# Start bytes of SBUF tiles within a 256-byte line, shifted for the inputs that TensorE streams through a four-layer fp32 network

## Chip, cores, metric

One core of one Trainium2 chip. The metric is device time in microseconds (us) of one execution, the median of several runs; lower is better.

## What is computed

Two layers of one kind and then two of another work on one sequence of 256 tokens with 1024 features. All tensors are float32. The matrix products are what costs time; cut to them, the reference is:

```python
# first kind of layer, DEPTH = 2
u = rms_norm(h, g_mix_pre)
(gq, gk, gv, gg, ra_f, ra_b, aq, ak, av, gate_a, gate_b) = jnp.split(u @ w_in, offsets, axis=-1)
branch_a = (o_gla * jax.nn.silu(gg)) @ w_o_gla
branch_b = gqa_attention(q, k, v) @ w_o_attn
mixed = jax.nn.sigmoid(gate_a) * branch_a + jax.nn.sigmoid(gate_b) * branch_b
h = h + rms_norm(mixed @ w_out, g_mix_post)
gate, up = jnp.split(rms_norm(h, g_ffn_pre) @ w_ffn_in, 2, axis=-1)      # 1024 -> 2 x 2816
h = h + rms_norm((jax.nn.silu(gate) * up) @ w_ffn_out, g_ffn_post)       # 2816 -> 1024
e = p_i @ w_ple_proj
h = h + rms_norm(jax.nn.sigmoid(h @ w_ple_gate) * e, g_ple_post)

# second kind of layer, DEPTH = 2
x = x + 0.5 * swiglu_ffn(rms_norm_2(x, ffn1_norm[i]), ffn1_w_in[i], ffn1_w_out[i])
proj = rms_norm_2(x, mix_norm[i]) @ w_in[i]
ya = (rg_lru(causal_dwconv(rx)) * jax.nn.gelu(rgate)) @ w_rnn_out[i]
yb = forgetting_attention(q, k, v, f_logit, ...) @ w_attn_out[i]
x = x + (jax.nn.sigmoid(ga + mb_a) * ya + jax.nn.sigmoid(gb + mb_b) * yb) @ w_o[i]
x = x + 0.5 * swiglu_ffn(rms_norm_2(x, ffn2_norm[i]), ffn2_w_in[i], ffn2_w_out[i])
x = x + jax.nn.sigmoid(rms_norm_2(x, ple_norm[i]) @ ple_w_gate[i] + ple_b_gate[i]) * (p[i] @ ple_w_proj[i])
```

## The kernel before

**Split products.** Every large product is computed in three matmuls of type float32r. Each operand is split into a rounded high part and a low remainder, and the kernel adds high x high, high x low and low x high. `weight` (L231) fetches 512 KB of weights into a tile `raw` and splits it into `hi` (ScalarE, L250) and `lo` (VectorE, L251), each 128 partitions x 1024 columns. Activations are split into pairs whose names end in h and l: `xTh`/`xTl` for a normalised input, `hh`/`hl` for the hidden units of an FFN, `oh`/`ol`, `yh`/`yl` and `mh`/`ml` in the mixers, `xrh`/`xrl` for the raw input of the last gate, `px` for the extra embedding.

**Two forms of product.** A matmul streams one operand (the moving one) past another that has been loaded into the array (the stationary one, 128 columns). In `gemm_fm` (L273, matmuls at L288 to L290) the weights are stationary and the activations move, 256 columns (1024 bytes of each partition) at a time. In `gemm_tm` (L297, matmuls at L315 to L317) the activations are stationary and the weights move, 512 columns at a time. Each matmul has a weight load of its own, and TensorE loads the stationary tile of the next matmul while the current one streams.

**Which layer uses which.** In the first two layers the FFN's first product is `gemm_fm` on `xT`, and the second is `gemm_tm` with `hh`/`hl` stationary. In the last two layers there are two FFNs each, both with `gemm_fm` in both products, so `hh`/`hl` move there. `layer_b` (L903) holds these four FFNs, `mixer_b` (L942) the mixer between them, `layer_a` (L518) the FFN of the first kind.

**Order.** Tiles are declared in pools, and a scheduling layer orders the instructions of each engine from dependencies and priorities. Nothing in this order is touched here.

**Where tiles start.** Pools are stacked in SBUF, and within a pool tiles follow each other. A tile's start byte in each partition is thus fixed when the program is built. `phase` (L212) puts a small unused tile at the head of a pool and pushes what follows by `n` bytes. Before the change, `act` (which holds `xT`) and `small` get 64 bytes each, and the pools of `layer_a`'s FFN and of `mixer_b` 32 bytes. With that, every moving or stationary activation pair starts at byte 0 of a 256-byte line (`px` at 224 in three places), while `raw`, `hi` and `lo` start at byte 192, all buffers of them. All these tiles are multiples of 256 bytes long, so each later block of them starts at the same byte of its line.

Of the kernel before, what the change touches and what calls it, by code (L numbers as in the profile page):

```python
# [11 lines left out]
F32 = mybir.dt.float32  # L12
# [6 lines left out]
P = 128  # L19
# [20 lines left out]
HOLD_B = 4  # L40
LAG = 3

X_PHASE = 64
POOL_PHASE = 32


class Norm:
# [3 lines left out]
    def __init__(self, net, g, tag="xT"):  # L51
        self.net, self.g = net, g
        self.xs = net.pair(net.act, tag)
        self.r = [None, None]
        self.R = net.act.tile([P, S], F32, tag="R", name=net.name("R"), bufs=2)
        self.ssq = [net.small.tile([P, 2], F32, tag="nssq", name=net.name("nssq")) for _ in range(2)]
# [124 lines left out]
class Net:  # L181
    def __init__(self, ctx, tc, a, raw_bufs=4, w_bufs=5, acc_bufs=3):
        self.tc = tc
        self.nc = tc.nc
        self.a = a
        pool = lambda name, bufs, **kw: ctx.enter_context(tc.tile_pool(name=name, bufs=bufs, **kw))
        psum = bass.MemoryType.PSUM
        self.const = pool("const", 1)
        self.wraw = pool("wraw", raw_bufs)
        self.whl = pool("whl", w_bufs)  # L190
        self.act = pool("act", 1)
        self.small = pool("small", 4)
        self.ps = pool("ps", acc_bufs, space=psum)
        self.pt = pool("pt", 2, space=psum)
        self.pm = pool("pm", 2, space=psum)
        self.pg = pool("pg", 1, space=psum)
        self.n = 0
        self.phase(self.act, X_PHASE)
        self.phase(self.small, X_PHASE)


        self.hold = self.held = None
        self.fetched = []
        nc = self.nc
        self.ident = self.const.tile([P, P], F32, name="ident")
        self.h = self.const.tile([P, 2, D], F32, name="h")
        self.expo = self.const.tile([P, 16], F32, name="expo")
        nc.vector.memset(self.expo, -0.5)
        self.ones = self.const.tile([P, P], F32, name="ones")
        nc.vector.memset(self.ones, 1.0)  # L210

    def phase(self, pool, n):  # L212

        pool.tile([P, n // 4], F32, tag="phase", name=self.name("phase"), bufs=1)

    def temporaries(self, ctx, bufs):
        self.tmp = ctx.enter_context(self.tc.tile_pool(name=self.name("tmp"), bufs=1))
# [300 lines left out]
def layer_a(net, i, nrm, following):  # L518
    nc, a, tc = net.nc, net.a, net.tc
    with ExitStack() as mx:  # L520
        nrm, px = mixer_a(net, i, mx, nrm)
    with tc.tile_pool(name=net.name("ffn"), bufs=1) as fp:
        net.phase(fp, POOL_PHASE)
        g_post = net.gain(a["g_ffn_post"][i])
        e = ple_proj(net, px, a["w_ple_proj"][i])
        raw = Raw(net, fp)
        net.ffn(nrm, a["w_ffn_in"][i], a["w_ffn_out"][i], net.post_norm(g_post, raw, fp, HOLD_FFN), fp)
        g_post = net.gain(a["g_ple_post"][i])
        nrm = following()
        px = ple_input(net, a["pT_2"][0]) if i + 1 == DEPTH else None  # L530

        def gated(tt, hf, acc):
            cs = slice(hf * 512, (hf + 1) * 512)
            t = net.t()
            nc.scalar.activation(t, acc, AF.Sigmoid)
            nc.vector.tensor_tensor(t, t, e[:, tt, cs], ALU.mult)
            return t

        net.gemm_tm(raw.xs, a["w_ple_gate"][i], net.post_norm(g_post, nrm, fp, HOLD_PLE if i + 1 < DEPTH else HOLD_LAST, gated), lag=LAG)
    return nrm, px  # L540


def ple_input(net, pT):
    with net.urgent(SPLIT_PRIO, 200):
        raw = net.t()
        net.nc.sync.dma_start(out=raw, in_=pT)
        px = (net.t((P, 2, S), F32R, "px"), net.t((P, 2, S), F32R, "px"))
        net.split_fm(raw, *px, 0)
    return px


def ple_proj(net, px, w):
    nc = net.nc
    e = net.t((P, 2, D), tag="e")
    net.gemm_tm(px, w, lambda tt, hf, acc: nc.scalar.copy(e[:, tt, hf * 512:(hf + 1) * 512], acc))
    return e
# [73 lines left out]
def flat(t):  # L630
    return t.rearrange("p a b -> p (a b)")


def blk(t, j):
    return t[:, 2 * j:2 * j + 2].rearrange("p a b -> p (a b)")
# [268 lines left out]
def layer_b(net, i, nrm, px, hT, following):  # L904
    nc, a, tc = net.nc, net.a, net.tc
    gains = a["gains"][i]
    gc = net.hp.tile([P, 48], F32, tag="gcols", name=net.name("gcols"), bufs=2)
    nc.sync.dma_start(out=gc, in_=gains)
    col = lambda k: gc[:, 8 * k:8 * k + 8]
    e = net.hp.tile([P, KB, S], F32, tag="e", name=net.name("e"))  # L910

    e_half = lambda px, q: net.gemm_fm(px, a["ple_w_proj_2"][i][q:q + 1], lambda j, acc: nc.scalar.copy(blk(e, 2 * q + j), acc), nkb=2)
    e_half(px, 0)
    with tc.tile_pool(name=net.name("ffn"), bufs=1) as fp:
        after = NormT(net, hT, col(1))
        net.ffn(nrm, a["ffn1_w_in_2"][i], a["ffn1_w_out_2"][i], net.add_scaled(hT, 0.5, after.blocks), fp, fm=True)
    with ExitStack() as cx:
        ms = mixer_b(net, i, cx, after)
        px = ple_input(net, a["pT_2"][i])
        nrm = NormT(net, hT, col(2))  # L920
        net.gemm_fm(ms, a["w_o"][i], net.add_scaled(hT, 1.0, nrm.blocks), tail=True)
    with tc.tile_pool(name=net.name("ffn"), bufs=1) as fp:
        e_half(px, 1)
        after = NormT(net, hT, col(3))
        net.ffn(nrm, a["ffn2_w_in_2"][i], a["ffn2_w_out_2"][i], net.add_scaled(hT, 0.5, after.blocks), fp, fm=True)
        nrm = following()
        px = ple_input(net, a["pT_2"][i + 1]) if i + 1 < DEPTH else None

        def epi(f, n, acc):
            t = net.t()[:, :n * S]  # L930
            net.times_r(t, acc, after)
            for c in range(n):
                nc.scalar.activation(t[:, c * S:(c + 1) * S], t[:, c * S:(c + 1) * S], AF.Sigmoid, bias=col(4)[:, f + c:f + c + 1])
            nc.vector.tensor_tensor(t, t, flat(e[:, f:f + n]), ALU.mult)
            nc.vector.tensor_tensor(flat(hT[:, f:f + n]), flat(hT[:, f:f + n]), t, ALU.add)
            nrm.blocks(f, n)

        net.gemm_fm(after.xs, a["ple_w_gate_2"][i], epi, tail=True)
    return nrm, px


def mixer_b(net, i, cx, nrm):  # L942
    nc, a, tc = net.nc, net.a, net.tc
    p1 = cx.enter_context(tc.tile_pool(name=net.name("mx"), bufs=1))
    net.phase(p1, POOL_PHASE)
    big = lambda tag, dt=F32: p1.tile([P, KB, S], dt, tag=tag, name=net.name(tag))
    fl = lambda t: t.rearrange("p a b -> p (a b)")
    xs, rs = nrm.xs, nrm.r
# [143 lines left out]
def _build(tc, a, out):  # L1092
    with ExitStack() as ctx:
        net = Net(ctx, tc, a)
        nc = tc.nc
        with ExitStack() as part:
            net.temporaries(part, T_BUFS_A)
            net.split = SPLIT_A
            nrm = lambda pool: first_norm(net, pool)
            nxt = [lambda: Norm(net, net.gain(a["g_mix_pre"][1])), lambda: Norm(net, net.gain(a["ffn1_norm_2"][0]))]  # L1100
            for i in range(DEPTH):
                nrm, px = layer_a(net, i, nrm, nxt[i])

        hp = ctx.enter_context(tc.tile_pool(name="hT", bufs=1))
        net.hp = hp
        net.temporaries(ctx, T_BUFS_B)
        net.split = SPLIT_B
        hT = hp.tile([P, KB, S], F32, name="hT")
        for tt in range(2):
            for hf in range(2):  # L1110
                ps = net.pt.tile([P, 4, P], F32, tag="pt", name=net.name("pt"))
                for j in range(4):
                    kb = hf * 4 + j
                    nc.tensor.transpose(ps[:, j], net.h[:, tt, kb * P:(kb + 1) * P], net.ident)
                nc.scalar.copy(hT[:, hf * 4:hf * 4 + 4, tt * P:(tt + 1) * P], ps)
        gc = hp.tile([P, 16], F32, name="gc")
        nc.sync.dma_start(out=gc, in_=a["gains_last"])
        nxt = [lambda: NormT(net, hT, gc[:, 0:8]), lambda: NormT(net, hT, gc[:, 8:16], out)]
        for i in range(DEPTH):
            nrm, px = layer_b(net, i, nrm, px, hT, nxt[i])  # L1120
# [140 lines left out]
```

## Time and profile before

| | us |
|---|---|
| median of 3 runs | 2344.41 |
| the 3 runs | 2346.03, 2344.41, 2343.48 |
| the profiled execution's own time | 2343.55 |
| its span, first to last instruction | 2341.8 |
| TensorE matmuls busy (16892) | 2291.4 |
| weight loads busy (16892) | 2168.4 |
| VectorE busy | 1600.6 |
| ScalarE busy | 1335.3 |
| GpSimd busy | 440.3 |

The span is 1.75 us shorter than the profiled execution's own time. A matmul's busy time of some 280 ns contains the pipeline behind the array and overlaps its successor, so the rate at which TensorE works is read from the distance between the starts of successive matmuls.

### The profile page before, as it was taken

The numbers are of one execution on the slowest core, as the hardware profiler recorded it, in microseconds if no ns is written. First come the engines' busy times: TensorE is split into PE (matmuls) and PEld (weight loads), VectorE is DVE, ScalarE is ACT, GpSimd is POOL, SyncE is SP. The second block draws the span as 40 slices with busy tenths as digits, with TensorE's granted clock in tenths as the row PEclk, the third lists the DMA queues.
The fourth block names the chain that finished last, engine by engine and source line by source line (L and its number), as shares of the span: only waits on it lengthen the run. The fifth ranks groups of instructions, "written<-read, shape, count | busy, mean of one in ns | idle before, by whom it ended". The sixth has DMA issues, their size and how long they took to land.

```text
span 2341.8 us, 42188 instructions
## 1 busy us (share of the span) xinstructions
PE 2291.4 (98%) x16892; PEld 2168.4 (93%) x16892; DVE 1600.6 (68%) x2133; ACT 1335.3 (57%) x2105; POOL 440.3 (19%) x443
## 2 busy tenths in 40 slices
PE   7999999998999999999999999999999999999997
PEld 6899899777899998799999899999999998999997
DVE  7876766477867765766586867665765677766655
ACT  6875554467764644554457765444644457755444
POOL 5222211064302110211001302110111103112101
PEclk9999999999999999999999999999999999999999
DMA  7445566554455666555665545666566655556662
GB/s 250 147 153 160 179 203 186 178 164 148 145 162 173 204 189 185 171 168 187 187 183 184 158 150 185 185 193 187 174 188 184 187 186 166 152 168 191 189 184 96
DMA packets 117102, 411.53 MB, mean 176 GB/s; under 512 B 14114, under 2 KB 16546, under 8 KB 116906
## 3 DMA queue, kind: packets, MB, share of 16 engines
q1 hardware_dynamic: 116906, 408.84, 56.2%
q8 instruction: 133, 2.18, 0.4%
q14 instruction: 63, 0.52, 0.1%
HBM read 407.74 MB, written 1.05 MB: 175 GB/s over the span
## 4 chain that ended last, share of the span: by engine, by line
PE 89%; DVE 4%; POOL 2%; issue 2%; ACT 1%; DMA 1%; SPq 0%; DVEq 0%; POOLq 0%; ACTq 0%
PE acc L290 22%; PE acc L289 22%; PE acc L288 22%; PE acc L315 6%; PE acc L316 6%; PE acc L317 6%; DVE lo L251 2%; PE sc L582 1%; PE po L593 1%; PE gs L890 1%; ACT hi L250 1%; POOL t L713 1%; POOL tab L689 0%; PE sc L606 0%; POOL hg L75 0%
## 5 line engine op out<-in xcount | busy, mean ns | idle before, releaser
L251 DVE TENSOR_TENSOR lo<-raw,hi 128x512 fp32r<-128x512 f32 (+1 forms) x1062 | 983.2, 952 | 439.5 <-ACT hi L250 437.4
L250 ACT ACTIVATE hi<-raw 128x512 fp32r<-128x512 f32 (+1 forms) x1062 | 824.3, 808 | 761.4 <-PE acc L289 396.1
L288 PE MATMUL acc<-xTh,hi 128*128 128x256 f32 x3296 | 924.3, 281 | 10.3 <-ACT t L1060 7.2
L289 PE MATMUL acc<-xTl,hi 128*128 128x256 f32 x3296 | 927.3, 282 | 0.7 <-DVE xTl L130 0.5
L290 PE MATMUL acc<-xTh,lo 128*128 128x256 f32 x3296 | 926.4, 281 | 0.0
L288 PEld LDWEIGHTS acc<-xTh,hi 128*128 128x128 f32 x3296 | 620.1, 188 | 12.5 <-ACT t L1060 7.7
L289 PEld LDWEIGHTS acc<-xTl,hi 128*128 128x128 f32 x3296 | 622.6, 189 | 2.6 <-DVE xTl L130 1.5
L290 PEld LDWEIGHTS acc<-xTh,lo 128*128 128x128 f32 x3296 | 621.3, 189 | 0.4
L396 POOL TENSOR_TENSOR t<-t,R 128x512 f32<-128x512 f32 x66 | 105.0, 1590 | 612.5 <-ACT t L394 612.5
L290 PE MATMUL acc<-hh,lo 128*128 128x256 f32 x704 | 197.1, 280 | 0.0
L288 PE MATMUL acc<-hh,hi 128*128 128x256 f32 x704 | 196.4, 279 | 0.0
L289 PE MATMUL acc<-hl,hi 128*128 128x256 f32 x704 | 196.4, 279 | 0.0
L315 PE MATMUL acc<-hi,xTh 128*128 128x512 f32 x416 | 165.7, 404 | 5.9 <-ACT hi L250 5.9
L316 PE MATMUL acc<-lo,xTh 128*128 128x512 f32 x416 | 167.4, 402 | 2.1 <-DVE lo L251 2.0
L317 PE MATMUL acc<-hi,xTl 128*128 128x512 f32 x416 | 166.4, 401 | 0.1
L289 PEld LDWEIGHTS acc<-hl,hi 128*128 128x128 f32 x704 | 132.4, 188 | 0.0
L290 PEld LDWEIGHTS acc<-hh,lo 128*128 128x128 f32 x704 | 132.1, 188 | 0.0
L288 PEld LDWEIGHTS acc<-hh,hi 128*128 128x128 f32 x704 | 131.6, 187 | 0.0
L315 PEld LDWEIGHTS acc<-hi,xTh 128*128 128x128 f32 x416 | 78.9, 190 | 23.4 <-ACT hi L250 6.0
L316 PEld LDWEIGHTS acc<-lo,xTh 128*128 128x128 f32 x416 | 79.1, 190 | 21.0 <-DVE lo L251 3.8
L317 PEld LDWEIGHTS acc<-hi,xTl 128*128 128x128 f32 x416 | 78.9, 190 | 18.7 <-DVE xTl L351 0.8
L379 DVE TENSOR_TENSOR t<-acc,R 128x512 f32<-128x512 f32 (+1 forms) x84 | 56.8, 676 | 44.1 <-PE acc L290 44.1
(321 smaller groups left out, 3236.5 us busy)
## 6 DMA issues: line engine op xcount, KB each, us to landing
raw<-ffn_w_in SPq DMA_DIRECT2D x176, 512.0 KB, 3.7
raw<-w_ffn_in SPq DMA_DIRECT2D x88, 512.0 KB, 4.3
raw<-ffn_w_out SPq DMA_DIRECT2D x88, 512.0 KB, 3.6
raw<-w_ffn_out SPq DMA_DIRECT2D x44, 512.0 KB, 4.1
raw<-w_gate SPq DMA_DIRECT2D x32, 512.0 KB, 3.6
raw<-w_gab SPq DMA_DIRECT2D x32, 512.0 KB, 3.7
raw<-w_gqk SPq DMA_DIRECT2D x16, 512.0 KB, 4.0
raw<-w_gv SPq DMA_DIRECT2D x16, 512.0 KB, 3.2
```

Of the source, the lines that this page charges most:

```text
L250: nc.scalar.activation(hi[:, cs], raw[:, cs], AF.Copy)
L251: nc.vector.tensor_tensor(lo[:, cs], raw[:, cs], hi.bitcast(F32)[:, cs], ALU.subtract)
L288: nc.tensor.matmul(o, lhsT=hi[:, cs], rhs=xh[:, kb], start=kb == 0, stop=False)
L289: nc.tensor.matmul(o, lhsT=hi[:, cs], rhs=xl[:, kb], start=False, stop=False)
L290: nc.tensor.matmul(o, lhsT=lo[:, cs], rhs=xh[:, kb], start=False, stop=kb == nkb - 1)
L315: nc.tensor.matmul(o, lhsT=xh[:, kb, ts], rhs=hi[:, cs], start=kb == 0, stop=False)
L316: nc.tensor.matmul(o, lhsT=xh[:, kb, ts], rhs=lo[:, cs], start=False, stop=False)
L317: nc.tensor.matmul(o, lhsT=xl[:, kb, ts], rhs=hi[:, cs], start=False, stop=kb == 2 * n - 1)
L379: self.nc.vector.tensor_tensor(v(out), v(acc), r, ALU.mult)
L396: nc.gpsimd.tensor_tensor(tb, tb, nrm.R.unsqueeze(1).to_broadcast([P, 2, S]), ALU.mult)
L582: nc.tensor.matmul(sc[:, j], lhsT=q_t[:, hp * 2 + j, tt * P:(tt + 1) * P], rhs=k_t[:, hp // 2], start=True, stop=True)
L593: nc.tensor.matmul(out[:, j], lhsT=v(jt, hp // 2), rhs=p_t[:, jt], start=jt == 0, stop=jt == 1)
```

## The change

The paddings at the heads of the pools get new sizes, and the pools of `layer_b`'s four FFNs, which had none, get one of 192, 160, 32 and 0 bytes.

```diff
-X_PHASE = 64
-POOL_PHASE = 32
+ACT_PHASE = 192
+SMALL_PHASE = 64
+FFN_A_PHASE = 96
+MIX_B_PHASE = 32
+FFN_B_PHASE = (192, 160, 32, 0)
...
-        self.phase(self.act, X_PHASE)
-        self.phase(self.small, X_PHASE)
+        self.phase(self.act, ACT_PHASE)
+        self.phase(self.small, SMALL_PHASE)
...
-        pool.tile([P, n // 4], F32, tag="phase", name=self.name("phase"), bufs=1)
+        if n:
+            pool.tile([P, n // 4], F32, tag="phase", name=self.name("phase"), bufs=1)
...
 def layer_a(net, i, nrm, following):
-        net.phase(fp, POOL_PHASE)
+        net.phase(fp, FFN_A_PHASE)
...
 def layer_b(net, i, nrm, px, hT, following):
     with tc.tile_pool(name=net.name("ffn"), bufs=1) as fp:
+        net.phase(fp, FFN_B_PHASE[2 * i])
         after = NormT(net, hT, col(1))
...
     with tc.tile_pool(name=net.name("ffn"), bufs=1) as fp:
+        net.phase(fp, FFN_B_PHASE[2 * i + 1])
         e_half(px, 1)
...
 def mixer_b(net, i, cx, nrm):
-    net.phase(p1, POOL_PHASE)
+    net.phase(p1, MIX_B_PHASE)
```

The start bytes within a 256-byte line, as the allocator gives them in the two programs:

| tiles | role | before | now |
|---|---|---|---|
| `hi`, `lo`, `raw` | weights | 192 | 192 |
| `xTh`, `xTl` | moving in `gemm_fm`, stationary in `gemm_tm` | 0 | 128 |
| `oh`, `ol`, `yh`, `yl`, `mh`, `ml` | the same | 0 | 128 |
| `hh`, `hl`, `xrh`, `xrl` in `layer_a` | stationary | 0 | 192 |
| `hh`, `hl` in the four FFNs of `layer_b`, in order | moving | 0, 0, 0, 0 | 64, 32, 160, 128 |
| `px` | both | 224 or 0 | 96 or 128 |
| `t`, `sq`, `e`, `R` and the like | VectorE, ScalarE, GpSimd | 0, 224, 160 | 128, 96, 32 |

On all five engines the instructions stand in the same order as before, with the same waits; every transfer has the same size and source.

## Rows read from the trace of the kernel before

**Rows 1.** The page: its head and busy time by engine (1).

```profile
span 2341.8 us, 42188 instructions
PE 2291.4 (98%) x16892; PEld 2168.4 (93%) x16892; DVE 1600.6 (68%) x2133; ACT 1335.3 (57%) x2105; POOL 440.3 (19%) x443
```

**Rows 2.** The page: the chain that ended last, by engine (4).

```profile
PE 89%; DVE 4%; POOL 2%; issue 2%; ACT 1%; DMA 1%; SPq 0%; DVEq 0%; POOLq 0%; ACTq 0%
```

**Rows 3.** Granted TensorE clock of the core, mean over the span.

```profile
core 0: 2341.8 us, clock 0.992
```

**Rows 4.** Stretches: us, busy (x count) PE, PEld, DVE, ACT, POOL; PEclk, DMA share, GB/s.

```profile
410.00:465.00 55.00, 55.00 (x237) 44.33 (x236) 25.87 (x40) 23.20 (x42) 0.43 (x2) 1.00 0.56 179
1090.00:1190.00 100.00, 100.00 (x852) 100.00 (x851) 58.53 (x58) 45.81 (x54) 11.43 (x8) 1.00 0.62 188
2250.00:2300.00 50.00, 50.00 (x426) 50.00 (x426) 28.70 (x29) 23.87 (x29) 4.44 (x4) 1.00 0.62 185
```

**Rows 5.** Matmul groups by shape: xcount | busy us, mean ns | idle before.

```profile
L288 PE MATMUL acc<-xTh,hi 128*128 128x256 f32 x3296 | 924.3, 281 | 10.3 <-ACT t L1060 7.2 <-ACT t L699 3.0
L288 PE MATMUL acc<-hh,hi 128*128 128x256 f32 x704 | 196.4, 279 | 0.0
L315 PE MATMUL acc<-hi,xTh 128*128 128x512 f32 x416 | 165.7, 404 | 5.9 <-ACT hi L250 5.9
L288 PE MATMUL acc<-oh,hi 128*128 128x256 f32 x256 | 71.2, 281 | 0.0
L315 PE MATMUL acc<-hi,hh 128*128 128x512 f32 x176 | 66.3, 395 | 0.0
L288 PE MATMUL acc<-yh,hi 128*128 128x256 f32 x128 | 35.9, 280 | 0.0
L288 PE MATMUL acc<-mh,hi 128*128 128x256 f32 x128 | 35.2, 280 | 0.0
L315 PE MATMUL acc<-hi,xrh 128*128 128x512 f32 x64 | 25.2, 398 | 0.0
L315 PE MATMUL acc<-hi,mh 128*128 128x512 f32 x64 | 24.3, 396 | 0.0
```

**Rows 6.** Timeline, PE, layer_b's first FFN: start, us; first and last of 28.

```profile
1103.76 0.28 PE L288 MATMUL acc<-xTh,hi 128*128 128x256 f32 x1
...
1106.94 0.28 PE L288 MATMUL acc<-xTh,hi 128*128 128x256 f32 x1
```

**Rows 7.** Timeline, PE, layer_b's mixer: first and last of 21.

```profile
1386.13 0.28 PE L288 MATMUL acc<-yh,hi 128*128 128x256 f32 x1
...
1388.40 0.28 PE L290 MATMUL acc<-yh,lo 128*128 128x256 f32 x1
```

**Rows 8.** Timeline, PE, px at byte 224: first and last of 21.

```profile
988.33 0.28 PE L289 MATMUL acc<-px,hi 128*128 128x256 f32 x1
...
990.66 0.28 PE L288 MATMUL acc<-px,hi 128*128 128x256 f32 x1
```

**Rows 9.** Timeline, PE, moving and stationary both at byte 0, and the next matmul.

```profile
72.87 0.40 PE L831 MATMUL z<-ra,up 98*128 98x256 f32 x2
73.11 0.28 PE L288 MATMUL acc<-xTh,hi 128*128 128x256 f32 x1
...
1978.40 0.63 PE L604 MATMUL sc<-right,left 104*128 104x512 f32 x2
1978.87 0.29 PE L288 MATMUL acc<-xTh,hi 128*128 128x256 f32 x1
```

**Rows 10.** Timeline, PE, 512 columns, layer_a's FFN: first and last of 16.

```profile
930.41 0.39 PE L316 MATMUL acc<-lo,hh 128*128 128x512 f32 x1
...
933.91 0.39 PE L316 MATMUL acc<-lo,hh 128*128 128x512 f32 x1
```

## The prediction
> **What bounds the kernel now.** I read the busy times first, then the chain of waits, then stretches of single products, and last the distance between matmuls. TensorE is busy for 98% of the span and its weight loads for 93%; VectorE has 68% and ScalarE 57% [rows 1]. The chain that ended last lies on TensorE for 89%, on VectorE for 4% [rows 2]. The clock is granted almost throughout, 0.992 in the mean, so it is at the upper of its two levels, 2.4 GHz [rows 3]. Idle time in front of the largest group is 10.3 us of 2342 [rows 5]. So TensorE does not wait for data. What can change its time is how fast one matmul follows another.
>
> That pace is remarkably even. In two FFNs of the last layers 852 matmuls start in 100 us and 426 in 50 us, at different shares of VectorE and ScalarE [rows 4]. In one of them 28 successive starts lie 1106.94 - 1103.76 = 3.18 us apart, 3.18 / 27 = 117.8 ns each [rows 6]. At 2.4 GHz 256 columns are 256 / 2.4 = 106.7 ns, so 11.1 ns of each are something else. With 512 columns it is (933.91 - 930.41) / 15 = 233.3 ns against 213.3 [rows 10]. The excess grows with the length of the stream (11 and 20 ns), although each matmul has one weight load in either case. It looks like reads of SBUF that hold each other up, by the stream alone or by stream and weight load together, and that is what the change acts on.
>
> A fixed tax is not all of it. In one stretch of the mixer the same instructions, with tiles at the same bytes of the line (0 moving, 192 stationary), run at (1388.40 - 1386.13) / 20 = 113.5 ns [rows 7]. So two paces exist for one and the same pair of addresses, each held for many matmuls. How stream and load stand to each other in time decides between them, and a shift of addresses should act like a shift in time.
>
> **The change part by part.** No instruction, wait or transfer is added or moved, so no queue has anything new in it. The cost is a difference in pace, times a number of matmuls. I call the moving tile's byte minus that of the stationary tile loaded meanwhile, modulo 256, its lead.
>
> *Activations moving past the weights (256 columns).* Counts are three times the first-term rows, since three terms run equally often: 3 x (3296 + 704 + 256 + 128 + 128) = 13536 [rows 5]. At 117.8 ns they are 1594 us, 68% of the span. The lead was 0 - 192 = 64 everywhere. It becomes 128 - 192 = 192 for all but three of the FFNs' `hh`/`hl`. Each of the four FFNs in the last layers has 704 / 4 x 3 = 528 such matmuls, so 13536 - 3 x 528 = 11952 get the lead 192, and 528 each get 128, 96 and 224.
>
> The trace of before shows no stream of 256 columns with the lead 192. Three nearest rows bound it. With lead 32 (`px` at 224) the pace is (990.66 - 988.33) / 20 = 116.5 ns [rows 8]. With lead 0 two matmuls take 73.11 - 72.87 = 0.24 us, 120 ns each [rows 9], a short and noisy row. The best pace seen is the 113.5 ns of the mixer. So the bounds of a matmul are -4.3 and +2.2 ns. I take 116.5 for lead 192, that is -1.3 ns. The reason is the products with 512 columns, whose lead is 192 - 0 = 192 now: 233.3 ns for twice the columns is 116.7 per 256, the same pace as with lead 32 and not that of lead 64 [rows 8, 10]. Two of the other leads thus agree on about 116.6, and the present one is the odd one. Gain: 1.3 x 11952 = 15.5 us, with bounds of -51.4 us (113.5) and +26.3 us (120).
>
> *The three FFNs at other bytes.* 1584 matmuls with leads of 128, 96 and 224. No row speaks for a sign. I take 0, between 1584 x -4.3 = -6.8 and 1584 x 2.2 = +3.5 us.
>
> *Weights moving past activations (512 columns).* 3 x (416 + 176 + 64 + 64) = 2160 matmuls [rows 5]. In the first layers' FFN and last gate, 3 x (176 + 64) = 720 of them, both tiles now start at byte 192, a lead of 0. The row with lead 0 at 512 columns is 0.47 / 2 = 235 ns [rows 9], +1.7 ns: +1.2 us. The other 1440 get the lead 64, the very one that costs most in the short stream; with 512 columns no row shows it. I take 0, with 1.7 ns either way, or 2.4 us.
>
> *VectorE, ScalarE, GpSimd.* Their tiles move by 128 bytes too. Were each of their instructions 1% slower or faster, VectorE's 4% of the chain would change by 0.04 x 0.01 x 2342 = 0.9 us; TensorE's work covers the rest, since VectorE is idle for a third of the span. I cost this at nothing. The cover is gone only if VectorE came near to 100% in a stage, and it has 29 of 50 us where the FFN is densest [rows 4].
>
> **Sum.** -15.5 + 0 + 1.2 + 0 = -14.3 us against the profiled execution's 2343.55, which is 0.86 below the median of the runs: 2343.55 - 14.3 = 2329. With the bounds of the two unsure terms added (-6.8 - 2.4, +3.5 + 2.4) this case alone reaches from 2320 to 2335.
>
> **A rule that speaks against any effect.** That equal work at equal addresses goes at 113.5 and at 117.8 ns is the row [rows 6, 7]. The Trainium skill, page "TensorE: Matmul & The Clock Gate", section "Step-by-step: what each phase is for", says that the moving operand and the weight load have independent read ports and that a weight load takes no bandwidth from a running matmul. By that rule a start byte changes nothing and the sum is 0, 2344 us. The two paces are not what one would expect from it, since neither data nor length differ, but they do not refute it, as the starting moment differs. The same page gives, under "Back-to-back issue gap", N / 2.4 + 2.5 ns; by it, as an estimate, all 256-column matmuls would pass at 109.2 ns and a layout that reached this would end near 2227 us. No row here is as fast.
>
> **The rivals.**
>
> *Nothing changes beyond 0.2%.* If what repeats is 128 bytes and not 256, leads of 64 and 192 are the same, and 11952 matmuls keep 117.8 ns. Then only the three FFNs and the 720 long ones are left, -6.8 + 1.2 to +3.5 + 1.2: 2338 to 2348, most likely 2344. The skill's rule of independent ports ends here as well. For it speaks that the paces of leads 32, 64 and 192 differ by 1% only. Against it: they differ.
>
> *Slower.* Stream and load meet earlier in the stream at lead 192 and hold each other up more often, at the pace of lead 0, 120 ns [rows 9]. Place: every 256-column product. Price: 2.2 x 13536 = 29.8 us, and 1.7 x 2160 = 3.7 us if the long ones go the same way: 2377. It decides as soon as the pace of `xT` is over 118.2 ns, since 0.4 x 11952 is 4.8 us. For it: 64 was a lead with one of the better rows, and half the circle away nothing is known. Against it: the long stream has the lead 192 and is no worse than its neighbours. Halfway it gives 2360.
>
> *Much faster.* The new leads put all products into the state of the mixer's good stretch, 113.5 ns [rows 7]: -51.4 us, or -58.2 with the three FFNs: 2292 to 2285. For it: the state exists and holds over 20 matmuls. Against it: it needs a relation in time, and with the present bytes nearly all stretches fall out of it [rows 4].
>
> That the change doesn't do what it says is excluded by the addresses of the built program.
>
> **How the numbers follow.** The forecast has a chance of 0.32, no change 0.24, slower 0.30, much faster 0.14. A measurement of this kernel tells about 0.2% or 4.7 us from no change. So faster by more is 0.32 + 0.14 = 0.46, the same 0.24, slower 0.30. Cases of both signs hold most of the chance, so beside the likeliest one's own 2320 to 2335 stands a wide range: up to 2370, which leaves out the last quarter of the slower case (about 0.08), and down to 2288, which leaves out the lower half of the much faster one (0.07).
>
> **What would show it.** Right: in the FFNs of the last layers about 858 matmuls of `xT` start in 100 us instead of 852 (100 / 0.1165), busy times and idle times of the other engines stay, the clock stays at 0.99. The four FFNs' second products show directly which leads are good, since nothing else differs between them. Wrong: 852 again for `xT` (a period of 128 bytes, or no effect); 840 or fewer (slower); 880 (the good state). The forecast's basis would also fall if the pace differed between stretches with equal leads, for then the moment of entry and not the address decides.

## Result and profile after

The changed kernel takes 2319.74 us in the median of four runs (2315.21 to 2323.19), the kernel before 2344.25 us beside it (four runs, 2343.48 to 2346.03). The ratio is 0.9893, with an interval of 0.9873 to 0.9913: 24.5 us faster. The forecast was 2329, range 2288 to 2370. The profiled execution is the fastest of the four, 2315.21 us, against 2343.55 us of the one before; the spans differ by 28.4 us.

The page of the kernel after (head, busy time by engine, the chain that ended last by engine, and the largest group of matmuls: count, busy us, mean ns, idle time in front):

```profile
span 2313.4 us, 42188 instructions
PE 2259.3 (98%) x16892; PEld 2145.3 (93%) x16892; DVE 1601.6 (69%) x2133; ACT 1334.2 (58%) x2105; POOL 441.3 (19%) x443
PE 88%; DVE 4%; POOL 3%; issue 2%; ACT 1%; DMA 1%; SPq 0%; DVEq 0%; POOLq 0%; ACTq 0%
...
L293 PE MATMUL acc<-xTh,hi 128*128 128x256 f32 x3296 | 921.7, 280 | 11.7 <-ACT t L1067 9.8
```

Nothing but TensorE's time has moved. VectorE, ScalarE and GpSimd are within 1.1 us of what they had [rows 1], the chain has the same make-up [rows 2], and a matmul still looks 280 ns long [rows 5]: its recorded length contains the pipeline and shows nothing of the pace. The granted clock differs by 0.002 [rows 3]:

```profile
core 0: 2313.4 us, clock 0.994
```

The pace is seen in stretches of a single product. First one stretch of the kernel before, from `xT` in `layer_a`'s first FFN (columns as in [rows 4]):

```profile
300.00:390.00 90.00, 90.00 (x767) 90.00 (x766) 56.33 (x90) 45.07 (x80) 10.97 (x8) 1.00 0.64 194
```

The same view of the kernel after. The first row is the same product, the second is `xT` in `layer_b`'s first FFN, and the other four are `hh` in its four FFNs, with leads of 128, 96, 224 and 192:

```profile
300.00:390.00 90.00, 90.00 (x796) 90.00 (x796) 58.47 (x93) 47.12 (x84) 10.66 (x8) 1.00 0.67 198
1000.00:1100.00 100.00, 100.00 (x851) 100.00 (x851) 61.00 (x62) 46.57 (x54) 16.06 (x9) 1.00 0.63 188
1110.00:1160.00 50.00, 50.00 (x424) 50.00 (x423) 28.16 (x27) 22.33 (x27) 2.83 (x2) 1.00 0.63 188
1560.00:1610.00 50.00, 50.00 (x419) 50.00 (x418) 28.21 (x28) 23.88 (x29) 4.41 (x4) 1.00 0.59 182
1775.00:1825.00 50.00, 50.00 (x425) 50.00 (x424) 29.05 (x29) 23.18 (x29) 3.71 (x4) 1.00 0.60 188
2220.00:2270.00 50.00, 50.00 (x427) 50.00 (x426) 28.60 (x29) 23.44 (x29) 3.06 (x3) 1.00 0.63 189
```

At one lead, 192, `xT` runs at two paces: 796 matmuls in 90 us in `layer_a`, 851 in 100 us in `layer_b`, where before it was 852 in a like stretch [rows 4]. Taken from all start times in ns, whole products sit at 113.3 or at 117.8 ns per matmul and hardly one between. I call these the **fast pace** and the **slow pace**. Both FFNs of `layer_a` went fast, and not one FFN of `layer_b`; the mean of all `xT` matmuls is 115.71 ns, against 117.75 before. The `hh` rows show a third thing: lead 96 is the worst of the four, 419 in 50 us, and leads 128 and 224 lie between it and lead 192 at its slow pace.

The long stream got faster where it was to get slower. TensorE's timeline of the kernel after (start, us, then the instruction), first and last of 16 successive matmuls in `layer_a`'s FFN, both tiles at byte 192 (lead 0):

```profile
433.67 0.39 PE L322 MATMUL acc<-hi,hl 128*128 128x512 f32 x1
...
437.07 0.39 PE L322 MATMUL acc<-hi,hl 128*128 128x512 f32 x1
```

That is 3.40 / 15 = 226.7 ns, where it was 233.3 [rows 10].

The same timeline, at an interruption of the stream in front of `layer_b`'s mixer:

```profile
1426.43 0.28 PE L293 MATMUL acc<-xTh,hi 128*128 128x256 f32 x1
...
1427.96 0.28 PE L294 MATMUL acc<-xTl,hi 128*128 128x256 f32 x1
1428.09 0.50 PE L157 MATMUL pss<-ones,sq 128*128 128x1 f32 x4
1428.45 0.37 PE L295 MATMUL acc<-xTh,lo 128*128 128x256 f32 x1
1428.65 0.28 PE L293 MATMUL acc<-xTh,hi 128*128 128x256 f32 x1
...
1429.24 0.28 PE L295 MATMUL acc<-xTh,lo 128*128 128x256 f32 x1
...
1430.94 0.28 PE L295 MATMUL acc<-xTh,lo 128*128 128x256 f32 x1
```

In front of the row `pss` there are 14 starts in 1.53 us, 1.53 / 13 = 117.7 ns. Behind it, from 1429.24 on, there are 16 in 1.70 us, 113.3 ns. Between the two lies the sum of squares of a norm, two short matmuls in full float32 (the row counts four records). Where such a matmul cuts in, the pace can change; in between it holds, as long as the lead stays. Tiles, addresses and order are the same on both sides.

A change of lead can do the same without any interruption. In `layer_b`'s first FFN `hh` (lead 128) hands over to `xT` (lead 192) with no other matmul between:

```profile
1168.82 0.28 PE L295 MATMUL acc<-hh,lo 128*128 128x256 f32 x1
1168.94 0.28 PE L293 MATMUL acc<-xTh,hi 128*128 128x256 f32 x1
...
1169.63 0.28 PE L293 MATMUL acc<-xTh,hi 128*128 128x256 f32 x1
...
1172.24 0.28 PE L295 MATMUL acc<-xTh,lo 128*128 128x256 f32 x1
```

The 24 starts from 1169.63 to 1172.24 are 2.61 / 23 = 113.5 ns apart, although this FFN's `xT` ran at the slow pace before `hh`.

### The profile page after: what moved, and what is told of

Same layout as the page of the kernel before. It is cut to its first block, busy times and chain, and to the rows that moved or that the text cites. A ratio compares the mean times of both kernels' runs of the same rounds, so it can differ in the third digit from the quotient of the medians.

```text
span 2313.4 us, 42188 instructions
## 1 busy us (share of the span) xinstructions
PE 2259.3 (98%) x16892; PEld 2145.3 (93%) x16892; DVE 1601.6 (69%) x2133; ACT 1334.2 (58%) x2105; POOL 441.3 (19%) x443
## 4 chain that ended last, share of the span: by engine, by line
PE 88%; DVE 4%; POOL 3%; issue 2%; ACT 1%; DMA 1%; SPq 0%; DVEq 0%; POOLq 0%; ACTq 0%
PE acc L294 22%; PE acc L293 22%; PE acc L295 22%; PE acc L321 5%; PE acc L320 5%; PE acc L322 5%; DVE lo L256 1%; POOL t L718 1%; ACT hi L255 1%; PE sc L587 1%; PE po L598 1%; PE gs L895 1%; PE sc L611 0%; POOL hg L79 0%; DMA gq<-g_q_norm 0%
```

## Experiments

Each kernel differs from the changed one (or, where it says so, from the one before) by what its diff shows. Paces are means over all steady steps, from the start times in ns; a row of a stretch stands where a verdict rests on it.

### All moving tiles at one byte

```diff
-FFN_B_PHASE = (192, 160, 32, 0)
+FFN_B_PHASE = (0, 0, 0, 0)
```

> All four FFN pools of the last layers without padding, so that hh and hl start at byte 128 like every other moving tile (lead 192); the rest as in the changed kernel. Theory A (two states, 113.3 and 117.8 ns, of which a stretch holds one from its entry on): the three moved FFNs leave 118.7, 120.0 and 118.3 ns for one of the two states, most likely the 117.8 that their xT product holds when it hands over; gain 528 x (0.9 + 2.2 + 0.5) = 1.9 us, up to 528 x 3 x 5.7 = 9 us if they enter the fast one. xT in the first layers' FFNs stays at 113.3 and in the last layers' FFNs at 117.8. Theory B (each lead has one pace of its own, the mean over all stretches at lead 192, 115.7 ns): the three go to 115.7, gain 528 x (3.0 + 4.3 + 2.6) = 5.2 us, and xT shows other paces from stretch to stretch only by chance.

Measured: 2319.8 us (2314.07 to 2322.8), ratio to before 0.9899 [0.9879, 0.9919]. The stretches of `hh` in the first two FFNs; those of the other two have 426 and 427 too:

```profile
1110.00:1160.00 50.00, 50.00 (x427) 50.00 (x426) 27.60 (x29) 22.90 (x28) 1.65 (x2) 1.00 0.61 189
1560.00:1610.00 50.00, 50.00 (x426) 50.00 (x426) 27.68 (x29) 23.23 (x28) 2.82 (x2) 1.00 0.60 189
```

All four run at 117.78 ns, the slow pace, and not at the mean of `xT`, 115.7. So lead 192 has no pace of its own in between. By paces the three other bytes of the change cost 528 x (0.89 + 2.22 + 0.56) = 1.9 us; the medians differ by 0.1 us, less than the runs of either kernel differ among themselves. The diversity of bytes is thus no part of the gain.

### The long stream's stationary tiles alone

From the kernel before, only `layer_a`'s FFN pool is padded, so that `hh` and `xr` start at byte 192, as the weights do:

```diff
+FFN_A_PHASE = 224
...
-        net.phase(fp, POOL_PHASE)
+        net.phase(fp, FFN_A_PHASE)
```

> The kernel before with one thing of the change: the FFN pool of the first layers is padded by 224 bytes, so that hh, hl and xrh, xrl, which are stationary there, start at byte 192 like the weights that stream past them (lead 0 instead of 192). All 256-column products keep byte 0. Theory A (the lead of a 512-column stream sets its pace): these 720 matmuls go from 233.4 to 226.7 and 227.8 ns, gain 528 x 6.7 + 192 x 5.7 = 4.6 us, 0.2%; every 256-column stretch stays at 117.5. Rival (the pace of these products follows the state of the 256-column stretch that hands over to them, which was the fast one in the changed kernel): they stay at 233 ns and the time does not move.

Measured: 2339.66 us (10 runs), ratio 0.9981 [0.9972, 0.9991]. The two stretches of [rows 4] that were 237 and 852:

```profile
410.00:465.00 55.00, 55.00 (x245) 45.54 (x244) 25.86 (x40) 23.49 (x43) 0.43 (x2) 1.00 0.57 185
1090.00:1190.00 100.00, 100.00 (x851) 100.00 (x850) 58.72 (x60) 46.31 (x55) 10.48 (x9) 1.00 0.58 186
```

`hh` went from 233.34 to 226.79 ns and `xr` from 233.3 to 227.6; every other product kept its mean within 0.2 ns. By paces that is 528 x 6.55 + 192 x 5.7 = 4.6 us, as expected; measured are 2.85 us, with an interval of 2.1 to 6.6. The lead sets the pace of the long stream too, and lead 0 is its best.

### Four other leads on the same product

```diff
-FFN_B_PHASE = (192, 160, 32, 0)
+FFN_B_PHASE = (64, 224, 96, 128)
```

> The changed kernel with other paddings in the four FFN pools of the last layers: hh and hl at bytes 192, 96, 224 and 0, leads of 0, 160, 32 and 64. It measures the leads that the other kernels do not. Theory A: lead 64 at 117.5 as in the kernel before; lead 32 near 116.7 as px had it; lead 0 about 120; lead 160 between 117.5 and 120 like its neighbours 128 and 224 (118.7 and 118.3). Sum 528 x (120 + 119 + 116.7 + 117.5) = 249.8 us, against 528 x (118.7 + 120.0 + 118.3 + 117.8) = 250.7 us in the changed kernel: the same time within 0.1%. Rival (the lead does not matter for hh, the hand-over state does): all four at 117.8.

Measured: 2316.1 us (2311.75 to 2317.72), ratio 0.9882 [0.9868, 0.9897]. `hh` in the four FFNs, leads 0, 160, 32, 64:

```profile
1110.00:1160.00 50.00, 50.00 (x419) 50.00 (x418) 26.98 (x27) 22.08 (x27) 1.57 (x2) 1.00 0.60 184
1560.00:1610.00 50.00, 50.00 (x424) 50.00 (x423) 28.02 (x27) 22.50 (x27) 2.82 (x2) 1.00 0.59 188
1775.00:1825.00 50.00, 50.00 (x431) 50.00 (x431) 28.33 (x28) 23.07 (x27) 2.82 (x2) 1.00 0.62 188
2220.00:2270.00 50.00, 50.00 (x427) 50.00 (x426) 28.26 (x27) 22.30 (x27) 2.83 (x2) 1.00 0.61 189
```

With the changed kernel this makes eight leads of one product. The paces found in all kernels, in ns:

| lead | 0 | 32 | 64 | 96 | 128 | 160 | 192 | 224 |
|---|---|---|---|---|---|---|---|---|
| 256 columns | 120.0 | 116.7 or 117.8 | 117.8 or 113.3 | 120.0 | 118.7 | 118.7 | 117.8 or 113.3 | 118.3 |
| 512 columns | 226.7 to 228.3 | - | 228.9 to 230.2 | 233.4 | - | - | 233.35 | 232.9 to 233.3 |

Where two values are joined by "or", a stretch holds one of them. The ranges are means of different products. Leads 96, 128, 160 and 224 were seen with 256 columns in one or two long stretches each, so a second pace is not excluded there.

### Everything at byte 192

```diff
-ACT_PHASE = 192
+ACT_PHASE = 0
...
-FFN_A_PHASE = 96
+FFN_A_PHASE = 32
...
-FFN_B_PHASE = (192, 160, 32, 0)
+FFN_B_PHASE = (0, 0, 0, 0)
```

> Every activation pair, moving or stationary, at byte 192 like the weights: lead 0 in all products of 256 and 512 columns. Theory A: 13536 matmuls of 256 columns at the 120 ns of the short rows with lead 0, against a mean of 116.2 in the changed kernel: +51 us; 2160 of 512 columns at 226.7 against 228.9: -5 us; sum about 2365 us, slower than the kernel before. Rival (lead 0 is best whichever tile moves, as it was for 512 columns): 256 columns at 113.3, 2160 at 226.7: 2319.7 - 39 - 5 = 2276 us.

Measured: 2360.63 us (2360.42 to 2360.83), ratio 1.0075 [1.006, 1.009]. Lead 0 in the long stream and in the short one:

```profile
410.00:440.00 30.00, 30.00 (x134) 24.84 (x133) 15.43 (x25) 13.22 (x24) 0.22 (x1) 1.00 0.53 176
1130.00:1180.00 50.00, 50.00 (x419) 50.00 (x418) 26.93 (x26) 21.28 (x25) 1.41 (x1) 1.00 0.61 186
```

Lead 0 is best with 512 columns (226.8 ns for `hh`) and, with lead 96, worst with 256 (120.0). There is one pace only: of the stretches of 20 matmuls and more none goes under 118 ns. The runs differ by 0.4 us where those of the changed kernel differ by 8. This is the slower case of the prediction, at another lead than it named.

### Weights and activations shifted together

```diff
+        self.phase(self.whl, 128)
```

> The changed kernel with 128 more bytes of padding ahead of the split weights and of all that follows: hi and lo at byte 64, xT and the other moving tiles at 0, hh at 192, 160, 32 and 0. Every lead is what it was, no absolute byte is. If the lead alone counts: the same paces product by product (120.0, 118.7, 118.3 for three hh, 113.3 and 117.8 for xT, 226.7 with lead 0) and the time of the changed kernel, 2320 us within 4. If the absolute byte of the moving tile counts (byte 0, as in the kernel before): xT at 117.8 throughout and some 2335 us or more.

Measured: 2320.47 us (2318.11 to 2328.2), ratio 0.992 [0.9894, 0.9945]. `xT` in `layer_a`'s second FFN, `xT` in `layer_b`'s first, `hh` in its second:

```profile
770.00:870.00 100.00, 100.00 (x852) 100.00 (x851) 63.95 (x101) 52.84 (x93) 11.99 (x9) 1.00 0.62 199
1000.00:1100.00 100.00, 100.00 (x885) 100.00 (x884) 63.80 (x66) 49.02 (x56) 16.06 (x9) 1.00 0.61 193
1560.00:1610.00 50.00, 50.00 (x419) 50.00 (x418) 27.41 (x27) 22.57 (x27) 2.82 (x2) 1.00 0.58 184
```

The split weights and all activations have moved by 128 bytes, every lead is the same, and so are the paces: `hh` has 118.7, 120.0, 118.3 and 117.8 ns in the four FFNs, as in the changed kernel. So it is the distance that counts, not the byte. But which products of lead 192 are fast has changed: here `layer_b`'s first FFN is, and `layer_a`'s second is not. Which one falls into the fast pace is not a property of the lead alone.

### Lead 32 everywhere

```diff
-ACT_PHASE = 192
+ACT_PHASE = 32
...
-FFN_A_PHASE = 96
+FFN_A_PHASE = 0
...
-FFN_B_PHASE = (192, 160, 32, 0)
+FFN_B_PHASE = (0, 0, 0, 0)
```

> Every moving activation at byte 224, a lead of 32 past the weights at 192; the stationary tiles of the first layers' FFN stay at 192. If a lead has a pace of its own: 256 columns at 116.7 ns in every stretch, without the two states of lead 192, 13536 x 1.1 = 14.9 us less than the kernel before, 720 long ones another 4.5 us, the other 1440 long ones at 232.9: 2342.5 - 14.9 - 4.5 - 0.7 = 2322 us. If lead 32 has two states as lead 192 has: stretches at 113.3 beside others at about 118, and a time that varies by some us from run to run.

Measured: 2325.74 us (2325.18 to 2326.24), ratio 0.9936 [0.9913, 0.9959]. `hh` in the first and the last FFN:

```profile
1110.00:1160.00 50.00, 50.00 (x431) 50.00 (x431) 28.49 (x28) 22.93 (x28) 3.17 (x2) 1.00 0.59 189
2235.00:2285.00 50.00, 50.00 (x431) 50.00 (x430) 29.20 (x29) 23.86 (x29) 4.44 (x4) 1.00 0.59 188
```

All four `hh` run at 116.67 ns, and the runs differ by 1.1 us. But lead 32 has two paces as well. `xT` in `layer_a`'s first FFN, at the same lead:

```profile
300.00:390.00 90.00, 90.00 (x766) 90.00 (x766) 56.02 (x88) 45.35 (x80) 10.93 (x9) 1.00 0.63 194
```

Here and in `layer_a`'s second FFN, 1054 matmuls each, a step is 117.78 ns, and the mean of all `xT` is 116.99. That is 0.32 x 9888 = 3.2 us of the 3.7 us by which the time lies over the expected 2322. No stretch of this kernel reached 113.3 ns. It is 6 us behind the changed kernel, whose two paces average lower and whose long stream is faster. Between this kernel and the one with everything at byte 192 nothing differs but start bytes, and they lie 2360.63 - 2325.74 = 34.9 us apart. The Trainium skill, page "TensorE: Matmul & The Clock Gate", section "Step-by-step: what each phase is for", gives the moving operand and the weight load independent read ports; by that rule the two would take the same time. The measured 34.9 us speak against it.

### An extra float32 matmul in four FFNs

On top of the kernel with all moving tiles at one byte, an unread float32 matmul of 128 columns cuts into the first product of each FFN of `layer_b`, at four places each:

```diff
-    def gemm_fm(self, xs, w, epi, nkb=KB, tail=False):
+BREAKS = ((6, 14, 22, 30), (6, 14, 22, 30), (6, 14, 22, 30), (6, 14, 22, 30))
+    def gemm_fm(self, xs, w, epi, nkb=KB, tail=False, breaks=()):
...
+                    if u // 8 in breaks:
+                        brk = self.pg.tile([P, P], F32, tag="pg", name=self.name("brk"))
+                        nc.tensor.matmul(brk, lhsT=self.ones, rhs=hi.bitcast(F32)[:, :P], start=True, stop=True)
```

> The kernel with all moving tiles at byte 128, and in the first product of each of the last layers' four FFNs four extra float32 matmuls of 128 columns whose result nobody reads, after the 6th, 14th, 22nd and 30th weight tile. Each costs about 0.2 us, 16 of them 3 us, if nothing else happens. Theory A (the state is drawn at each interruption by a float32 matmul, and a stretch keeps it): the xT stretches of these FFNs no longer stand at 117.8 from end to end but change to 113.3 and back at the extra matmuls, about every second one ending in the fast state; where the last one ends fast, hh goes at 113.3 too. At half fast: 4 x 1400 x 4.4 / 2 = 12 us gained, 9 us net, some 2311 us. Theory C (the state belongs to the product or the layer, for instance to the tiles' place in SBUF beyond the 256-byte line): these FFNs stay at 117.8 and the time rises by 3 us.

Measured: 2307.89 us (2302.09, 2319.48, 2312.22, 2303.56), ratio 0.9866 [0.9829, 0.9903]. TensorE's timeline at the second such matmul of the first FFN; 16 starts stand from the first row to the second, 17 in the last two:

```profile
1025.30 0.28 PE L299 MATMUL acc<-xTh,lo 128*128 128x256 f32 x1
...
1027.06 0.28 PE L299 MATMUL acc<-xTh,lo 128*128 128x256 f32 x1
1027.18 0.38 PE L295 MATMUL brk<-hi,ones 128*128 128x128 f32 x2
1027.32 0.36 PE L297 MATMUL acc<-xTh,hi 128*128 128x256 f32 x1
1027.52 0.28 PE L298 MATMUL acc<-xTl,hi 128*128 128x256 f32 x1
...
1028.11 0.28 PE L297 MATMUL acc<-xTh,hi 128*128 128x256 f32 x1
...
1029.92 0.28 PE L298 MATMUL acc<-xTl,hi 128*128 128x256 f32 x1
```

Stretches of the same kernel, `xT` in `layer_a`'s second FFN and `hh` in `layer_b`'s first:

```profile
770.00:870.00 100.00, 100.00 (x852) 100.00 (x851) 63.83 (x101) 52.40 (x92) 11.98 (x9) 1.00 0.62 197
1110.00:1160.00 50.00, 50.00 (x444) 50.00 (x443) 29.41 (x30) 24.33 (x29) 2.83 (x2) 1.00 0.62 195
```

In front of the extra matmul it is 1.76 / 15 = 117.3 ns, behind it 1.81 / 16 = 113.1 ns. It costs 0.22 us: from 1027.06 to 1027.52 are 0.46 us where two steps would be 0.24. Of the 16, nine met the fast pace and kept it, four turned slow into fast, three left it slow, and none turned fast into slow. From the second one on all four FFNs were fast, through `hh`, at 113.33 ns. So the slow pace isn't the lead's price. The runs differ by 17 us. The granted clock, 0.991 to 0.993, does not sort them. Presumably the products without extra matmuls still fall either way, as `layer_a`'s second FFN was slow in this profile and fast in that of the changed kernel; with one profiled execution of each kernel this is not shown.

### The same extra matmuls in the kernel before

> The kernel before, lead 64 throughout, with the same 16 extra float32 matmuls (four in the first product of each of the last layers' FFNs). Theory A with a lead that decides how likely the fast state is: at lead 64 nearly every interruption was followed by 117.8 ns (of the longer stretches in the profile of before only a handful of some 20 matmuls ran at 113.3), so the FFNs stay at 117.8 and the time rises by the 16 matmuls, about 3 us, to 2345 or 2346. Rival (the extra matmuls bring the fast state by themselves, whatever the lead): about half of these stretches go to 113.3 as they did at lead 192, and the time falls by 10 to 25 us.

Measured: 2324.86 us (2323.26 to 2326.62), ratio 0.9931 [0.9915, 0.9947]. `xT` and `hh` in `layer_b`'s first FFN, at lead 64:

```profile
1000.00:1100.00 100.00, 100.00 (x875) 100.00 (x875) 62.05 (x64) 52.48 (x64) 17.14 (x11) 0.99 0.61 193
1130.00:1180.00 50.00, 50.00 (x444) 50.00 (x443) 30.01 (x30) 24.07 (x30) 4.45 (x4) 1.00 0.63 195
```

I had expected 3 us more, and it was 16.7 less, as the rival had it: a miss. My theory was that at lead 64 hardly any interruption brings the fast pace. For the extra matmul it fell. At lead 64 the extra matmul brings the fast pace as well (four of ten times from slow, and six of six times it was kept), and all four `hh` products ran at 113.33 ns. With `xT` down from 117.75 to 116.53 ns and `hh` by 4.45, less 16 x 0.22, the paces give 9888 x 1.22 + 2112 x 4.45 - 3.5 = 17.9 us, about what was measured.

What the lead changes are the odds at the interruptions that the program has anyway. I count neighbouring stretches of at least 20 matmuls that lie at most 3 us apart. At lead 64, in the kernel before, slow turned fast 5 of 59 times and fast was kept 0 of 5 times. At lead 192, in the changed kernel, slow turned fast 11 of 25 times and fast was kept 20 of 39. In the kernel shifted by 128 bytes, with the leads of the changed one, it was 13 of 38 and 7 of 28. So the odds of getting fast go with the lead, and those of staying fast with something else too. The two layers of a kind repeat each other almost step for step, so the independent cases are fewer than these counts.

### Extra matmuls in all six FFNs

From the kernel with all moving tiles at one byte: the same matmul at five places of the first product of every FFN, and at two places of the second product of every gated sum.

```diff
+BREAKS = (2, 4, 6, 8, 16)
+BREAKS_MIX = (1, 3)
...
-        self.gemm_fm(nrm.xs, wi, e)
+        self.gemm_fm(nrm.xs, wi, e, breaks=BREAKS)
...
-    net.gemm_fm(xb, wb, epi)
+    net.gemm_fm(xb, wb, epi, breaks=BREAKS_MIX)
```

> All moving tiles at byte 128, with 38 extra float32 matmuls: after the 2nd, 4th, 6th, 8th and 16th weight tile of the first product of all six FFNs, and after the 1st and 3rd of the second half of each mixer's gated sum. Theory A: a stretch that starts at 117.8 gets several draws early on, and one that runs at 113.3 mostly keeps it, so all six FFNs run at 113.3 from the 8th tile at the latest, the first layers' FFNs in every execution and not in most alone. Against the kernel with 16: the stretch up to the 14th tile is shorter by some 200 matmuls x 4.4 ns = 0.9 us in each of four FFNs, the products after the gated sums gain up to 370 x 4.4 = 1.6 us in each of two layers, and 22 more matmuls cost 0.22 us each, 4.8 us: about the same median, 2305 us, but less spread between runs than the 17 us seen there (2302.1 to 2319.5). If the draw is even and not in favour of the fast state, about half the FFNs end slow: 2312 to 2320 us.

Measured: 2297.48 us (five runs, 2296.72 to 2299.64), ratio 0.9814 [0.98, 0.9828]. `xT` in `layer_a` and in `layer_b`, and `hh`:

```profile
300.00:390.00 90.00, 90.00 (x796) 90.00 (x796) 58.27 (x92) 46.28 (x83) 11.19 (x9) 1.00 0.63 200
1000.00:1100.00 100.00, 100.00 (x885) 100.00 (x884) 63.02 (x65) 47.92 (x55) 16.06 (x9) 1.00 0.61 193
1110.00:1160.00 50.00, 50.00 (x443) 50.00 (x443) 29.65 (x29) 23.18 (x28) 2.83 (x2) 1.00 0.60 196
```

All six FFNs are fast, `xT` has 113.92 ns in the mean, and the runs differ by 3 us. Of 38 extra matmuls 32 kept the fast pace, two brought it, and four, all in the gated sums of `layer_b`, left it slow. By paces against the changed kernel: 9888 x 1.79 + 2112 x 5.37 less 38 x 0.22 is 20.7 us; measured are 22.3. I had expected about 2305. This beats both kernels, the one before by 44.1 us (2341.53 beside it), although it does more work.

## Why the prediction was right, point by point

| term | forecast, us | by measured paces, us |
|---|---|---|
| 11952 short ones at lead 192 | -15.5 | -22.3 (`xT` -20.2, `oh` -1.4, `yh` -0.7, others 0) |
| three `hh` products | 0 | +1.9 |
| 720 long ones at lead 0 | +1.2 | -4.6 |
| 1440 long ones at lead 64 | 0 | -5.7 |
| sum | -14.3 | -30.7 |

The paces are those of the profiled executions, whose spans differ by 28.4 us; the 2.3 us between the sum and that I did not follow further (idle time in front of the largest group is 1.4 us longer). The median of the runs, 24.5 us better, lies between the forecast's and the profile's gain; 2319.74 us is just outside the 2320 to 2335 that the forecast's own case reached. That the sum came out near is partly luck: a third of the gain, 10.3 us of 30.7, lies in the long stream, which was put at a loss of 1.2 us, and the reason for the largest term was wrong.

**The bound, TensorE's pace: right.** Busy and idle times of the others stayed, as "what would show it" had it, and where the paces of an experiment were added up they gave its time to within the spread of its runs. The two stretches of [rows 4], read as pace "at different shares of VectorE and ScalarE", differ little in them (VectorE 58.5% and 57.4%); that these engines make no difference stands on the steps counted in the last section.

**The term of `xT`: right in sign, mis-sized, and with the wrong picture.** "I take 116.5 for lead 192, that is -1.3 ns": the mean was -2.04, and it is a mean of 113.3 and 117.8, with 47% of the matmuls at the fast pace. The test of 858 in 100 us met nowhere; product by product it was 796 in 90 us, which is 884 in 100 (the "much faster" rival), or 851 ("nothing changes"). The prediction had both paces before it [rows 6, 7] and named the case: "the moment of entry and not the address decides". That is half of what the runs showed: the entry decides product by product, and the address sets how often an entry from the slow pace goes well, 5 of 59 times at lead 64 and 11 of 25 at lead 192.

**The reason given for 116.5: wrong.** It took the long stream's pace at lead 192, halved, for the short stream's. The two lengths do not rank the leads alike: lead 0 is best for 512 columns and, with lead 96, worst for 256.

**The 720 long ones: wrong sign.** "The row with lead 0 at 512 columns is 0.47 / 2 = 235 ns": that row [rows 9] is the step behind a product of another shape (104 rows) and says nothing of a steady stream. It is 226.7 ns, 6.6 less than before; alone, from the kernel before, it brought 2.85 us. **The 1440 others: wrong.** Taken as 0 within 2.4 us, they gained 3.9 ns (`xT`) and 4.5 ns (`m`) each.

**The three `hh` products: in the bounds** (-6.8 to +3.5), on the bad side; lead 96, with 120.0 ns, is as bad as lead 0.

**The rivals.** A period of 128 bytes does not fit the other pairs of leads: 0 has 120.0 and 128 has 118.7, 32 has 116.7 or 117.8 and 160 has 118.7. For leads 64 and 192 the two paces do agree, and only the odds differ. The slower rival's price of a short matmul was right, and its place was not: 120 ns is what lead 0 costs in the short stream, and with everything there the time is 2360.63 us. That lead 192 would not share it was in no row of before. The Trainium skill's rule of independent ports, which ended at no change, is told of with the run at lead 32. That the gain by paces went 16.4 us past the forecast is not the much faster rival alone: 6.8 us come from the short matmuls, about half of which fell into the fast pace, and 11.5 us from the long stream, less 1.9 us for the three `hh`.

**What stays open.** At many interruptions the first step, into the next stretch, is 200 to 208 ns. I count those stretches of at least 20 matmuls. At lead 64 (the kernel before and the one with `layer_a`'s pool alone) 14 of the 36 with 200 or 201 went fast, and none of the 70 with more. At lead 192 (the changed kernel, and the two that move only `hh`) it is the other way about: 31 of the 86 with 200 or 201, and 72 of 74 with more. In the kernel shifted by 128 bytes, with the same leads, it is 16 of 32 with more, so this sorts the entries and doesn't explain them. The prediction said that the way in which stream and load stand to each other in time decides; no run shows that. What decides within these few nanoseconds, which resource is shared, and why the extra matmul never lost the fast pace (47 of 47 times) while the program's own interruptions often did, is left open; no run here tells it.

## What to carry to other kernels

When TensorE is busy throughout, read the distance between matmul starts, product by product, and not the mean over a group: a mean of two paces predicts neither. Where the pace of equal work differs, look for what stands at the change of pace; here the cheap lever was an extra matmul of 0.22 us at such a place, and the start bytes set the paces and loaded the dice. Do not carry a good offset from one stream length to another, and measure one over several runs: the kernels with `xT` at lead 192 and no extra matmuls in `layer_a` differed by 6 to 17 us from run to run, the one before by up to 8 us, and those at leads 0 and 32 by 0.4 and 1.1 us. That the two paces cause this spread is likely and not shown.

## What the runs showed of the hardware that was not expected

- The pace of float32r matmuls depends on the distance of the two tiles' start bytes, counted here modulo 256 (a longer period was not tested), and not on the bytes themselves: 113.3 to 120.0 ns for 256 columns, 226.7 to 233.4 ns for 512, at a granted clock of 0.99.
- At leads 64 and 192 there are two paces, 113.3 and 117.8 ns, and at lead 32 there are 116.7 and 117.8, each held over hundreds of matmuls. What VectorE and ScalarE do meanwhile makes no difference: in the kernel before a step is 117.7 ns where both are idle and 117.7 where both are busy.
- No steady stretch was faster than 113.3 ns. The Trainium skill, page "TensorE: Matmul & The Clock Gate", section "Back-to-back issue gap", has N / 2.4 + 2.5 ns for an isolated matmul, which is 109.2 as an estimate for 256 columns; no run here shows that.
